# Stores, small constants and weight folding around the modulation stage of a hybrid encoder layer

## The chip, the cores and the metric

The kernel runs on one core of a Trainium2 chip. The metric is the device time of one execution in microseconds. Of the kernel before there are three timed runs, with a median of 2102.57 us (2102.38 to 2103.07). A profiled execution is shown beside them.

The engines are named as the profile names them: PE is TensorE (matmuls; PEld its weight loads), DVE is VectorE, ACT is ScalarE, POOL is GpSimd, and SP is the engine that issues most transfers. A DMA issue of an engine is written SPq or POOLq.

## What is computed

The reference is one layer of an encoder, run for two sequences of 1024 rows and 1024 columns. Cut to what matters:

```python
mod = silu(c) @ w_ada + b_ada                       # w_ada is 1024 x 6144
sh1, sc1, ga1, sh2, sc2, ga2 = split(mod, 6)
h = rmsnorm(x, g_mix) * (1 + sc1) + sh1
z = h @ w_in                                        # q_lat 256, kv_lat 128, k_pe 64, f_in 512
mix = concat(mla(q_lat, kv_lat, k_pe), fourier(f_in)) @ w_out
x = x + ga1 * mix
h2 = rmsnorm(x, g_ffn) * (1 + sc2) + sh2
y = x + ga2 * ((silu(h2 @ w_gate) * (h2 @ w_up)) @ w_down)      # then a final rmsnorm
```

The latent attention uses w_uq (256 to 4 heads of 128 + 64), w_ukv (128 to 4 heads of 128 + 128) and the gains g_q_lat and g_kv_lat. The kernel folds these weights into each other first.

## The kernel before

The kernel works in stages, and the change lies in the first. Everything is float32; a product of two large operands is done as three matmuls (mm3, L78 to L80) of a rounded high part and a remainder, which split (L62, L63) makes with a copy on ACT and a subtraction on DVE.

**The modulation stage.** w_ada's columns for shift and scale of the first norm (2048 of them) are read in eight chunks of 128 rows, 1 MB each (mod_load, L207), and mod_mm (L216) multiplies each with silu(c) into one PSUM bank. Chunks 0, 1, 3, 4 and 7 go through two wada tiles, the others through tiles that later work uses under other names (hh0, hh1). When the eighth chunk is multiplied, mod_row (L221) copies the sum, mod_vecs (L144 to L156) transposes it and adds bias and gain with twelve small DVE operations, and the first shift and scale vectors (sh1, s1) are there. flip (L381, L384) then transposes the normalised rows of x and applies them on ACT: hf, split into hh and hl. Nothing of the main work can start before that.

Between the chunks the stage prepares weights:
- fold_q (L238, L239) multiplies parts of w_uq and w_ukv into wq, fold_pe (L258) adds the rotary columns, and wq is stored to DRAM (wq_d, L260, issued by POOL);
- fold_out (L251, L253) multiplies the value part of w_ukv with w_out for one head, in two halves; heads 0 and 1 here, stored to wo_d by POOL (L254);
- prep_wcs (L336 to L346) folds the Fourier part of w_in (wfT, four loads of 512 KB) with a constant table;
- wz_split splits the other part of w_in (two loads of 896 KB, wz0 and wz1);
- norm (L365, L368) of the first rows: squares on ACT, a reciprocal root on POOL (rstd, L102 to L109), the scaling on DVE.

Small constants come one by one: cmask, cT (the conditioning), gkvr (one row of 128 read for all 128 partitions), gq, bT, gT. silu(c) is stored to DRAM too (sc_d, L197, POOL).

**The pairs.** Then eight pairs of row blocks follow: zproj (two products with wz, its rotary part with the tables ropec and ropes), latents (transposes), fourier_in (two products with wcs), flip of the next pair, evenodd (sums and differences on POOL, L397), norm of the pair after next. A generator, extras, puts other work between their steps, one step at each next(more): the fold_out of heads 2 and 3 (its weights loaded with L244; stored by SP), then the eight chunks of w_ada's gate columns (mod_load, mod_mm), then the products with the gates.

**What sets the order.** A tile framework schedules the instructions of each engine; each engine works in its own order. SP's transfers use eight completion semaphores in turn, so that each transfer's issue waits for the landing of the one eight before it, and for whatever still uses the tile that it fills. A tile with a tag is one buffer under several names: wq lies in hl0, which later holds the first hl; wuqT in hh0. The pool of PSUM has eight banks, taken in turn.

The later stages (attention, output product, the feed-forward products) are not touched.

Of the kernel before, what the change touches and what calls it, by code (L numbers as in the profile page):

```python
# [21 lines left out]
P = 128  # L22
D = 1024
# [29 lines left out]
def hybrid_encoder_kernel(ctx: ExitStack, tc: tile.TileContext, a: dict):  # L53
# [39 lines left out]
    nc.sync.dma_start(cmask, a["cmask"])  # L93
# [49 lines left out]
    def mod_vecs(mr, bank, bT, gT, bcol, gi, sv, shv):  # L143
        pt = bank().rearrange("p (a b) -> p a b", a=4)  # L144
        for c in range(4):
            nc.tensor.transpose(pt[:, c, :], mr[:, c * P : (c + 1) * P], ident)
        for s in range(2):
            for j in range(2):
                nc.vector.tensor_tensor(
                    out=shv[s][:, 4 * j : 4 * j + 4], in0=pt[:, :, 32 * j + s],  # L150
                    in1=bT[:, bcol + 4 * j : bcol + 4 * j + 4], op=ALU.add)
                nc.vector.tensor_tensor(
                    out=sv[s][:, 4 * j : 4 * j + 4], in0=pt[:, :, 64 + 32 * j + s],
                    in1=bT[:, bcol + 8 + 4 * j : bcol + 12 + 4 * j], op=ALU.add)
            nc.vector.tensor_scalar(out=sv[s], in0=sv[s], scalar1=1.0, scalar2=None, op0=ALU.add)
            nc.vector.tensor_tensor(out=sv[s], in0=sv[s], in1=gT[:, gi, :], op=ALU.mult)  # L156
# [7 lines left out]
    with ExitStack() as st:  # L164
# [25 lines left out]
        cT = w.tile([P, NC, 2], F32, name="cT")  # L190
        scT = w.tile([P, NC, 32], F32, name="scT")
        bT = w.tile([P, 48], F32, name="bT")
        gT = w.tile([P, 2, NC], F32, name="gT")
# [30 lines left out]
        def fold_loads():  # L224
            wukT = w.tile([P, HEADS, KVL], F32, tag="lh", name="wukT", bufs=2)
            nc.sync.dma_start(wukT, a["wukT"])
            nc.sync.dma_start(wuqT, a["wuqT"])
            gkvr = w.tile([P, KVL], F32, tag="t1", name="gkvr", bufs=2)
            nc.sync.dma_start(gkvr, a["gkvr"].partition_broadcast(P))
            gq = w.tile([P, 3], F32, name="gq")  # L230
            nc.sync.dma_start(gq, a["gq"])
            return wukT, gkvr, gq

        def fold_q(wukT, gkvr, gq):
# [12 lines left out]
        def fold_out(h, wo2, wuvT, gq):  # L247
            for g in range(2):
                gs = slice(512 * g, 512 * g + 512)
                ps = bank()  # L250
                nc.tensor.matmul(ps, wuvT[:, h, :], wo2[:, h % 2, gs], start=True, stop=True)  # L251
# [4 lines left out]
        def fold_pe(wpe, gq):  # L256
# [3 lines left out]
            nc.gpsimd.dma_start(wq_d, wq)  # L260
# [11 lines left out]
        def extras():  # L272
# [97 lines left out]
        def flip(k, g):  # L370
# [11 lines left out]
            for c in range(2):  # L382
                cc = 2 * g + c
                nc.scalar.activation(hf[:, cc], pt[:, c], AF.Identity, bias=sh1[s][:, cc : cc + 1], scale=s1[s][:, cc : cc + 1])  # L384
# [84 lines left out]
        fq = fold_loads()  # L469
        gq = fq[2]  # L470
        wt = [mod_load(c, cols0, wada_tile()) for c in range(2)]
        fold_q(*fq)
# [3 lines left out]
        wo2 = wo_load(0, wide("hf", (P, 2, D)))  # L476
# [7 lines left out]
        for q in range(4):  # L484
            wf.append(w.tile([P, 4, 256], F32, tag=("eoh0", "eol0", "eoh1", "eol1")[q], name="wf", bufs=1))
            nc.sync.dma_start(wf[q], a["wfT"][:, :, 256 * q : 256 * q + 256])
        fold_out(0, wo2, wuvT, gq)
        fold_out(1, wo2, wuvT, gq)
        fold_pe(wpe, gq)
        mod_mm(0, 2, wt[0])  # L490
        mod_mm(0, 3, wt[1])
# [6 lines left out]
        wz0 = wz_load(0, wide("hf", (P, 4 * 512)))  # L498
        mod_mm(0, 4, wt[0])
# [5 lines left out]
        wf.clear()  # L505
# [3 lines left out]
        mod_vecs(mod_row(0), bank, bT, gT, 0, 0, s1, sh1)  # L509
# [8 lines left out]
        nc.sync.dma_start(ropec, a["ropec"])  # L518
        nc.sync.dma_start(ropes, a["ropes"])
# [1148 lines left out]
def _layout(i):  # L1668
# [10 lines left out]
    for s in range(2):  # L1679
# [5 lines left out]
        "cT": c.reshape(2, NC, P).transpose(2, 1, 0),  # L1685
# [3 lines left out]
        "wfT": w_in[:, DZ:].T.reshape(4, P, D).transpose(1, 0, 2),  # L1689
# [4 lines left out]
        "gq": np.concatenate([sq["g_q_lat"].reshape(2, P).T, sq["g_kv_lat"].reshape(KVL, 1)], 1), "gkvr": sq["g_kv_lat"],  # L1694
        "w4": w4t, "w_out": sq["w_out"], "wgu": wgu, "w_down": sq["w_down"], "g_final": np.asarray(i["g_final"]),
    }
    return {k: np.ascontiguousarray(v) for k, v in r.items()}
# [19 lines left out]
```

## Time and profile before

| | |
|---|---|
| median of three runs | 2102.57 us |
| profiled execution, whole | 2103.97 us |
| its span, first to last instruction | 2102.2 us |
| mean granted PE clock | 0.99 |
| PE busy over the span | 2035.1 us, 97% |
| read and written in HBM | 259.47 and 122.49 MB |

The span is what the profile's windows divide; 1.8 us of the execution lie around it. A row of the timeline has the start and the duration in us, the engine and line, the operation, the tiles (out<-in), shapes and count, and in brackets how long the engine stood idle before and what ended that. A float32 matmul counts twice in it. A row of the windows has the window, its length, then for PE, PEld, DVE, ACT and POOL the busy us and count, then the granted clock of PE (1.00 is full speed), the busy share of the 16 DMA engines and GB/s.

### The profile page before, as it was taken

The page shows a single profiled execution, that of the slowest core. Times are in us where ns is not written, and L with a number is a line of the kernel's source. Part 1 is how long each engine was busy: PE and PEld are TensorE (multiplying, and loading weights), DVE is VectorE, ACT ScalarE, POOL GpSimd, SP SyncE. Part 2 cuts the span into 40 slices and gives each one's busy share as a digit, 9 for nine tenths or more (in the row PEclk, how much of TensorE's full clock was granted, in tenths as well). Part 3 has the DMA queues.
Part 4 walks back from the last instruction along what each step waited for, and adds up shares of the span by engine and source line. Part 5 has one row for each costly group of instructions (what it writes and reads, how often), then busy time and mean ns, then how long its engine had stood idle before and what let it go on. Part 6 is the DMA issues. An engine that isn't in the chain of part 4 may idle for free. (4 is left out here: it accounts for less than half of the span.)

```text
span 2102.2 us, 28839 instructions
## 1 busy us (share of the span) xinstructions
PE 2035.1 (97%) x10044; PEld 1667.4 (79%) x10044; DVE 1403.6 (67%) x2088; ACT 902.3 (43%) x1764; POOL 832.7 (40%) x1027
## 2 busy tenths in 40 slices
PE   6999999999999989999999999999999999999998
PEld 3788777888888877888888888877788888888876
DVE  3657766766777667767677666776756566567674
ACT  2766534455555555233323355453233233336441
POOL 1555111111313314878778610334554454420142
PEclk8999999999999999999999999999999999999999
DMA  9685795544643465455455487674332232258672
GB/s 370 206 260 172 258 314 174 131 101 101 157 109 125 146 212 203 165 185 193 168 180 197 159 269 261 212 238 160 116 125 101 76 126 100 76 167 284 226 227 93
DMA packets 187103, 375.49 MB, mean 179 GB/s; under 512 B 19341, under 2 KB 60941, under 8 KB 183885
## 3 DMA queue, kind: packets, MB, share of 16 engines
q1 hardware_dynamic: 168460, 316.09, 45.1%
q0 software_dynamic: 18496, 57.55, 9.1%
q8 instruction: 79, 1.29, 0.3%
q14 instruction: 68, 0.55, 0.1%
HBM read 259.47 MB, written 122.49 MB: 182 GB/s over the span
## 5 line engine op out<-in xcount | busy, mean ns | idle before, releaser
L78 PE MATMUL bank<-H,wh 128*128 128x512 f32 x1232 | 492.7, 400 | 9.2 <-ACT val L1397 4.5
L80 PE MATMUL bank<-H,wl 128*128 128x512 f32 x1232 | 486.7, 395 | 1.9 <-DVE wl L63 1.9
L79 PE MATMUL bank<-H,wh 128*128 128x512 f32 x1232 | 485.0, 394 | 0.2 <-DVE H L63 0.2
L138 DVE TENSOR_TENSOR val<-bank,val 128x512 f32<-128x512 f32 x244 | 167.0, 689 | 194.9 <-PE bank L80 188.0
L78 PEld LDWEIGHTS bank<-H,wh 128*128 128x128 f32 x1232 | 232.0, 188 | 66.1 <-DVE val L138 5.9
L80 PEld LDWEIGHTS bank<-H,wl 128*128 128x128 f32 x1232 | 232.1, 188 | 62.4 <-DVE wl L63 2.6
L79 PEld LDWEIGHTS bank<-H,wh 128*128 128x128 f32 x1232 | 231.8, 188 | 55.7 <-DVE H L63 0.6
L63 DVE TENSOR_TENSOR wl<-draw,wh 128x512 fp32r<-128x512 f32 x286 | 201.9, 741 | 87.5 <-ACT wh L62 87.0
L62 ACT CAST wh<-draw 128x512 fp32r<-128x512 f32 x286 | 168.4, 619 | 159.9 <-PE bank L79 83.8
L138 POOL TENSOR_TENSOR val<-val 128x512 f32<-128x512 f32 x58 | 84.1, 1456 | 368.3 <-DVE val L1498 189.2
L79 PE MATMUL bank<-wl,wh 128*128 128x512 f32 x572 | 223.8, 391 | 3.2 <-DVE wl L63 3.2
L62 ACT CAST wh<-rgu 128x512 fp32r<-128x512 f32 x172 | 106.7, 621 | 270.7 <-PE bank L79 214.2
L78 PE MATMUL bank<-wh 128*128 128x512 f32 x572 | 222.7, 389 | 0.0
L80 PE MATMUL bank<-wh,wl 128*128 128x512 f32 x572 | 222.7, 389 | 0.0
L62 ACT CAST wh<-val 128x512 fp32r<-128x512 f32 x133 | 82.3, 622 | 279.3 <-PE bank L79 250.9
L63 DVE TENSOR_TENSOR wl<-val,wh 128x512 fp32r<-128x512 f32 x133 | 137.8, 1038 | 89.1 <-ACT wh L62 89.0
L135 POOL TENSOR_TENSOR val<-rgu 128x512 f32<-128x512 f32 x84 | 124.2, 1478 | 124.9 <-DMA rgu<-in_wgu_dram 105.4
L63 DVE TENSOR_TENSOR wl<-rgu,wh 128x512 fp32r<-128x512 f32 x172 | 165.3, 962 | 4.8 <-ACT wh L62 4.6
L79 PEld LDWEIGHTS bank<-wl,wh 128*128 128x128 f32 x572 | 107.3, 188 | 28.7 <-DVE wl L63 6.8
L78 PEld LDWEIGHTS bank<-wh 128*128 128x128 f32 x572 | 107.4, 188 | 23.0 <-ACT wh L62 0.3
L80 PEld LDWEIGHTS bank<-wh,wl 128*128 128x128 f32 x572 | 107.4, 188 | 21.9
L135 POOL TENSOR_TENSOR val<-val 128x512 f32<-128x512 f32 x89 | 120.1, 1366 | 1.3
(354 smaller groups left out, 4053.4 us busy)
## 6 DMA issues: line engine op xcount, KB each, us to landing
rgu<-in_wgu_dram SPq DMA_DIRECT2D x86, 512.0 KB
draw<-s_d SPq DMA_DIRECT2D x143, 256.0 KB
s_d<-val POOLq DMA_DIRECT2D x88, 256.0 KB, 4.0
draw<-t_d SPq DMA_DIRECT2D x88, 256.0 KB
s_d<-val SPq DMA_DIRECT2D x66, 256.0 KB
draw<-in_w_down_dram SPq DMA_DIRECT2D x55, 256.0 KB
wada<-in_w_ada_dram SPq DMA_DIRECT2D x13, 1024.0 KB
xt<-in_x_dram SPq DMA_DIRECT2D x16, 512.0 KB
```

The costliest lines, as they stand in the source:

```text
L62: here["a"] = nc.scalar.copy(hi, src).ins
L63: here["v"] = nc.vector.tensor_tensor(out=lo, in0=src, in1=rd(hi), op=ALU.subtract).ins
L78: nc.tensor.matmul(out, lh, rh, start=first, stop=False, skip_group_check=cont)
L79: nc.tensor.matmul(out, lh, rl, start=False, stop=False, skip_group_check=cont)
L80: here["t"] = nc.tensor.matmul(out, ll, rh, start=False, stop=last, skip_group_check=cont).ins
L135: return eng.tensor_tensor(out=out, in0=x, in1=y, op=ALU.subtract).ins
L138: eng.tensor_tensor(out=out, in0=x, in1=y, op=ALU.add)
```

## The change

All of it lies in the first stage.

- **Constants.** cT, gq, bT, gT and gkvr are laid side by side on the host (gkvr repeated for the 128 partitions) and come in one transfer, pk, 128 x 211 floats, third on SP's queue. cmask is loaded later.
- **Stores.** The stores of sc_d, wq_d and wo_d move from POOL's queue to SP's, behind the load of the eighth chunk: two of wo_d and wq_d ahead of wz1 and of the second pair's x, the other six of wo_d, ropec, ropes, sc_d and cmask behind.
- **Folds.** fold_out for heads 2 and 3 runs between the chunks; the second half of w_out is loaded ahead of the fourth chunk. extras loses these steps, so that each of its later steps comes one next(more) earlier. The eight results lie in tiles of their own until they are stored.
- **wfT** is laid out so that each of its four loads reads 4 KB runs, where it read 1 KB runs; the last two loads come after the fourth chunk's.
- **Vectors.** mod_vecs has six DVE operations in place of twelve (in both places that call it). One of the eight hf of the first pair is done on DVE instead of ACT.

```diff
-    nc.sync.dma_start(cmask, a["cmask"])
...
         for s in range(2):
-            for j in range(2):
-                nc.vector.tensor_tensor(
-                    out=shv[s][:, 4 * j : 4 * j + 4], in0=pt[:, :, 32 * j + s],
-                    in1=bT[:, bcol + 4 * j : bcol + 4 * j + 4], op=ALU.add)
...
+            for k, v in enumerate((shv[s], sv[s])):
                 nc.vector.tensor_tensor(
...
-            nc.vector.tensor_scalar(out=sv[s], in0=sv[s], scalar1=1.0, scalar2=None, op0=ALU.add)
-            nc.vector.tensor_tensor(out=sv[s], in0=sv[s], in1=gT[:, gi, :], op=ALU.mult)
+            nc.vector.scalar_tensor_tensor(out=sv[s], in0=sv[s], scalar=1.0, in1=gT[:, gi, :], op0=ALU.add, op1=ALU.mult)
...
+        pk = w.tile([P, 211], F32, name="pk")
...
-        nc.sync.dma_start(cT, a["cT"])
         nc.vector.memset(scT, 0.0)
-        nc.scalar.activation(scT[:, :, 0:2], cT, AF.Silu)
-        nc.gpsimd.dma_start(sc_d, scT)
...
             nc.sync.dma_start(wuqT, a["wuqT"])
-            nc.sync.dma_start(gkvr, a["gkvr"].partition_broadcast(P))
-            nc.sync.dma_start(gq, a["gq"])
+            nc.sync.dma_start(pk, a["pk"])
+            nc.scalar.activation(scT[:, :, 0:2], cT, AF.Silu)
...
-                so = stile("so")
-                nc.vector.tensor_scalar(out=so, in0=ps, scalar1=gq[:, 2:3], scalar2=None, op0=ALU.mult)
-                (nc.gpsimd if h < 2 else nc.sync).dma_start(wo_d[:, h, gs], so)
+                nc.vector.tensor_scalar(out=outs[g], in0=ps, scalar1=gq[:, 2:3], scalar2=None, op0=ALU.mult)
+                folded.append((wo_d[:, h, gs], outs[g]))
...
-            nc.gpsimd.dma_start(wq_d, wq)
...
             cols1 = [(2 * D, D), (5 * D, D)]
-            wo2 = wo_load(1, wada_tile().rearrange("p a b -> p (a b)").rearrange("p (a b) -> p a b", a=2))
-            yield
-            fold_out(2, wo2, wuvT, gq)
             wt = mod_load(0, cols1, wada_tile())
             yield
-            fold_out(3, wo2, wuvT, gq)
             yield
...
+                if k == 0 and cc == 1:
+                    nc.vector.tensor_scalar(out=hf[:, cc], in0=pt[:, c], scalar1=s1[s][:, cc : cc + 1],
+                                            scalar2=sh1[s][:, cc : cc + 1], op0=ALU.mult, op1=ALU.add)
+                    continue
...
-        wt = [mod_load(2, cols0, wide("hh1")), mod_load(3, cols0, wada_tile())]
+        wt = [mod_load(2, cols0, wide("hh1"))]
         nc.sync.dma_start(c2, a["c2"])
...
+        wf_load(0)
+        wf_load(1)
+        wo2.append(wo_load(1, wide("hl1", (P, 2, D))))
+        wt.append(mod_load(3, cols0, wada_tile()))
...
         for i in range(4):
             prep_wcs(i, wf[i // 2])
+        wf_load(2)
+        wf_load(3)
+        mod_mm(0, 3, wt[1])
         wt = [mod_load(4, cols0, wada_tile()), mod_load(5, cols0, wide("hh1"))]
-        nc.sync.dma_start(bT, a["bT"])
-        nc.sync.dma_start(gT, a["gT"])
+        fold_out(2, wo2[1], wuvT, (w.tile([P, 512], F32, tag="gah0", name="so"), stile("so")))
+        fold_out(3, wo2[1], wuvT, (stile("so"), stile("so")))
         norm(0)
         wz0 = wz_load(0, wide("hf", (P, 4 * 512)))
+        for i in range(4, 8):
+            prep_wcs(i, wf[i // 2])
...
         wt = [mod_load(6, cols0, wide("hh0")), mod_load(7, cols0, wada_tile())]
+        for dst, so in folded[:2]:
+            nc.sync.dma_start(dst, so)
+        nc.sync.dma_start(wq_d, wq)
         wz1 = wz_load(4, wide("hl1", (P, 4 * 512)))
-        for i in range(4, 8):
-            prep_wcs(i, wf[i // 2])
...
+        x_load(1)
+        for dst, so in folded[2:]:
+            nc.sync.dma_start(dst, so)
+        nc.sync.dma_start(ropec, a["ropec"])
+        nc.sync.dma_start(ropes, a["ropes"])
+        nc.sync.dma_start(sc_d, scT)
+        nc.sync.dma_start(cmask, a["cmask"])
         wz_split(0, wz0)
         mod_mm(0, 6, wt[0])
         mod_mm(0, 7, wt[1])
-        mod_vecs(mod_row(0), bank, bT, gT, 0, 0, s1, sh1)
+        mr = w.tile([P, 4, 256], F32, tag="eol1", name="modrow", bufs=1).rearrange("p a b -> p (a b)")[:, :512]
+        nc.vector.tensor_copy(mr, mods.pop(0))
+        mod_vecs(mr, bank, bT, gT, 0, 0, s1, sh1)
...
-        nc.sync.dma_start(ropec, a["ropec"])
-        nc.sync.dma_start(ropes, a["ropes"])
```

On each engine the instructions after this stage and its pairs come in the same order as before, but for a few neighbours that change places.

More of the change, by code (lines that the diff above doesn't have):

```diff
@@ L189, in hybrid_encoder_kernel @@
         zoc = [w.tile([P, NC, ZOW], F32R, name=f"zoc{i}") for i in range(2)]
-        cT = w.tile([P, NC, 2], F32, name="cT")
+        pk = w.tile([P, 211], F32, name="pk")
+        cT = pk[:, 0:16].rearrange("p (a b) -> p a b", b=2)
+        gq = pk[:, 16:19]
+        bT = pk[:, 19:67]
+        gT = pk[:, 67:83].rearrange("p (a b) -> p a b", a=2)
+        gkvr = pk[:, 83:211]
         scT = w.tile([P, NC, 32], F32, name="scT")
-        bT = w.tile([P, 48], F32, name="bT")
-        gT = w.tile([P, 2, NC], F32, name="gT")
-        nc.sync.dma_start(cT, a["cT"])
         nc.vector.memset(scT, 0.0)
-        nc.scalar.activation(scT[:, :, 0:2], cT, AF.Silu)
-        nc.gpsimd.dma_start(sc_d, scT)
         mods = {}
@@ L227, in fold_loads, with fold_q @@
             nc.sync.dma_start(wuqT, a["wuqT"])
-            gkvr = w.tile([P, KVL], F32, tag="t1", name="gkvr", bufs=2)
-            nc.sync.dma_start(gkvr, a["gkvr"].partition_broadcast(P))
-            gq = w.tile([P, 3], F32, name="gq")
-            nc.sync.dma_start(gq, a["gq"])
-            return wukT, gkvr, gq
-        def fold_q(wukT, gkvr, gq):
+            nc.sync.dma_start(pk, a["pk"])
+            nc.scalar.activation(scT[:, :, 0:2], cT, AF.Silu)
+            return wukT
+        def fold_q(wukT):
             for h in range(HEADS):
@@ L245, in wo_load, with fold_out @@
             return t
-        def fold_out(h, wo2, wuvT, gq):
+        folded = []
+        def fold_out(h, wo2, wuvT, outs):
             for g in range(2):
@@ L468, in hybrid_encoder_kernel @@
         cols0 = [(0, 2048)]
-        fq = fold_loads()
-        gq = fq[2]
+        wukT = fold_loads()
         wt = [mod_load(c, cols0, wada_tile()) for c in range(2)]
-        fold_q(*fq)
+        fold_q(wukT)
         nc.gpsimd.memset(lw, 0.0)
@@ L475, in hybrid_encoder_kernel @@
         nc.sync.dma_start(wuvT, a["wuvT"])
-        wo2 = wo_load(0, wide("hf", (P, 2, D)))
+        wo2 = [wo_load(0, wide("hf", (P, 2, D)))]
         wpe = w.tile([P, 2, HEADS * ROPE], F32, tag="lh", name="wpe", bufs=2)
```

27 lines of the change are left out of this document (14 added, 13 removed).

## Prediction

> **What bounds the kernel now.** I read the page first, then the busy time by stage, then what TensorE (PE) waited for.
>
> ```profile
> span 2102.2 us, 28839 instructions
> PE 2035.1 (97%) x10044; PEld 1667.4 (79%) x10044; DVE 1403.6 (67%) x2088; ACT 902.3 (43%) x1764; POOL 832.7 (40%) x1027
> ```
>
> PE is the bound over the whole, but 97% is an average. By stage (window, its length, busy us of PE, PEld, DVE, ACT, POOL, granted clock, DMA share, GB/s):
>
> ```profile
> 0.00:56.00 56.00, 34.67 (x173) 20.29 (x174) 19.14 (x59) 14.09 (x37) 6.39 (x20) 0.85 0.94 366
> 69.20:80.90 11.70, 7.22 (x35) 4.05 (x34) 9.13 (x21) 9.00 (x22) 9.58 (x25) 1.00 0.30 90
> 80.90:225.00 144.10, 143.26 (x912) 122.17 (x912) 94.51 (x188) 86.04 (x214) 74.86 (x157) 1.00 0.71 223
> 700.00:2102.00 1402.00, 1371.53 (x6029) 1111.55 (x6027) 943.73 (x1182) 537.36 (x953) 642.56 (x652) 0.99 0.51 174
> ```
>
> Two holes lie where the change works: 21.3 us without PE in the first 56, with the DMA share at 0.94, and 4.5 us between 69.2 and 80.9, with the DMA idle and three engines busy. From 80.9 PE is full (143.26 of 144.10), and late 98% full. So what PE is spared early ends up whole in the time. PE's longest wait in the first stage, from the waits (us, times, longest), and the matmuls of the last chunk, from the timeline (start, us):
>
> ```profile
> PE bank L216 <- DMA wide<-in_w_ada_dram: 7.6, 2, 6.2
> ```
>
> ```profile
> 48.63 1.93 PE L216 MATMUL bank<-wada,scT 128*32 128x512 f32 x8 [0.57 <-DMA wada<-in_w_ada_dram]
> ```
>
> The modulation's eighth chunk of w_ada landed at 48.63, and everything after hangs on it. The first stage is a queue of bytes ahead of that chunk, and I count what the change does to it. The DMA's rate in pieces of the stage, and the sizes (KB each) of what moves:
>
> ```profile
> 5.00:8.00 3.00, 1.62 (x6) 1.36 (x6) 0.00 (x0) 0.00 (x0) 0.53 (x1) 1.00 0.57 160
> 7.50:47.90 40.40, 26.93 (x138) 14.91 (x138) 16.31 (x43) 10.43 (x30) 4.45 (x11) 0.87 1.03 407
> 12.00:21.00 9.00, 7.86 (x22) 2.42 (x19) 2.25 (x5) 0.00 (x0) 1.08 (x2) 1.00 1.02 417
> 21.00:24.00 3.00, 3.00 (x19) 0.61 (x18) 0.91 (x2) 0.00 (x0) 1.10 (x2) 1.00 1.07 345
> 28.00:31.00 3.00, 1.71 (x14) 1.74 (x15) 0.50 (x3) 0.69 (x3) 0.00 (x0) 0.95 1.07 366
> 31.00:34.00 3.00, 3.00 (x16) 3.00 (x16) 1.76 (x7) 1.58 (x7) 0.00 (x0) 0.50 1.05 434
> 40.00:47.90 7.90, 1.77 (x8) 0.20 (x8) 3.00 (x4) 4.08 (x6) 1.73 (x6) 0.56 1.01 420
> ```
>
> ```profile
> wo_d<-so POOLq DMA_DIRECT2D x4, 256.0 KB, 7.7
> wada<-in_w_out_dram SPq DMA_DIRECT2D x1, 1024.0 KB
> wq_d<-wq POOLq DMA_DIRECT2D x1, 768.0 KB, 8.3
> sc_d<-scT POOLq DMA_DIRECT2D x1, 128.0 KB, 6.9
> ```
>
> **Part 1, bytes ahead of the last chunk: -2.3 us.** Four wo_d stores (1024 KB), wq_d (768) and sc_d (128) leave: 1920 KB. The second half of w_out (1024 KB), which came after the chunk, now comes before it. The small constants are a wash (six transfers of 109 KB against pk, 128 x 211 floats, 105.5 KB). Net -900 KB = 0.92 MB, at the 407 GB/s of 7.5 to 47.9: 2.3 us. The Trainium skill ("DMA: Bandwidth & Descriptors", section "Where 436 GB/s comes from") says that about 358 GB/s binds transfers between HBM and SBUF; by that the bytes would be worth 2.6 us. The trace disagrees, with 420 GB/s over 7.9 us.
>
> ```profile
> 0.73 0.39 SPq L93 DMA_DIRECT2D cmask<-in_cmask_dram  x1
> 1.63 0.43 SPq L226 DMA_DIRECT2D wukT<-in_wukT_dram  x1
> 2.58 0.43 SPq L229 DMA_DIRECT2D gkvr<-in_gkvr_dram  x1
> 3.53 0.91 SPq L207 DMA_DIRECT2D wada<-in_w_ada_dram  x2
> ```
>
> **Part 2, the start of the queue: -0.9 us.** SP spends 0.73 to 1.63 on cmask and cT before its first large load. In the changed order wukT is SP's first transfer.
>
> **Part 3, the hole behind gkvr: -1.4 us, between 0 and -1.85.** From 5 to 8 us the queue moved 160 GB/s with the engines 57% busy, although 1 MB loads had been issued since 3.53: 3 x (1 - 160/417) = 1.85 us lost. gkvr (one row read for 128 partitions) and gq stand there. They go; pk, contiguous per partition, takes their place. Whether they cause the hole no row proves, so 0 stays an end; I take three quarters.
>
> **Part 4, slow stretches: -0.5 us, between 0 and -0.9.** 21 to 24 (345) and 28 to 31 (366) lie below 417: 3 x (72 + 51)/417 = 0.9 us. In the first the stores mix with loads; in the second wfT is read in 1 KB runs, which become 4 KB.
>
> The chunk lands 5.1 us sooner (3.2 to 5.9). Waits in the queue: each SP transfer waits for the eighth before it to land, and a wada tile for PE's matmuls on what it held. At 2.5 us a MB the chunk before it in that tile is multiplied at some 30 us (rival 5), and the eighth chunk's turn comes at 38.8: I expect nothing to run dry. The folds of heads 2 and 3 now stand among these matmuls, on a PE that idles 21 us here; cost 0.
>
> **Part 5, behind the chunk.**
>
> ```profile
> 53.84 1.48 ACT L384 ACTIVATE hf<-bank,sh,s 128x256 f32<-128x256 f32 x3 [8.45 <-DVE s L152]
> 55.20 0.62 ACT L62 CAST hh<-hf 128x512 fp32r<-128x512 f32 x1
> 55.85 0.69 DVE L63 TENSOR_TENSOR hl<-hf,hh 128x512 fp32r<-128x512 f32 x1 [1.64 <-ACT hh L62]
> 55.87 0.47 PE L78 MATMUL bank<-wz_h,hh 128*128 128x448 f32 x1 [0.50 <-ACT hh L62]
> 57.12 1.80 ACT L62 CAST wz_h<-wide 128x896 fp32r<-128x896 f32 x2
> 61.72 1.09 ACT L365 ACTIVATE junk<-xt 128x1024 bf16<-128x1024 f32 x1
> ```
>
> Twelve small DVE operations become six, and one of the eight hf moves from ACT (1.48/3 = 0.49 us) to DVE, which waited 1.64 there. The first s is then the fourth of these operations instead of the eighth: I take **-0.5 us** (0 to -0.8).
>
> The stores moved behind the chunk now precede wz1 and x(1). 512 + 768 KB at the mixed 345 GB/s are 3.8 us, wz1 (896 KB) 2.2, x(1) 2.5. Counted from the chunk, wq_d lands at +3.8, wz1 at +6.0, x(1) at +8.5. They are needed at +6.7 (hl shares wq's tile: 55.85 - 48.63 - 0.5), +8.0 (57.12) and +12.6 (61.72): covered, by 2.0 us at the tightest. The other six stores, ropec and ropes come behind; the first use of ropec, after zproj, is 2 us later still. Cost 0, and each us beyond the cover costs one.
>
> **Part 6, the folds that leave 69 to 81.**
>
> ```profile
> 55.29 0.89 SPq L355 DMA_DIRECT2D xt<-in_x_dram  x2
> 74.63 0.22 POOL L102 TENSOR_SCALAR rs_v<-ms 128x2 f32<-128x2 f32 x1
> 74.93 1.88 PE L251 MATMUL bank<-wada,wuvT 128*128 128x512 f32 x4
> 76.55 0.19 POOL L109 TENSOR_TENSOR rs_r<-rs_w,rs_y 128x2 f32<-128x2 f32 x1
> 77.96 1.88 PE L251 MATMUL bank<-wada,wuvT 128*128 128x512 f32 x4
> 80.83 0.39 PE L78 MATMUL bank<-wcs_h,eoh 128*128 128x256 f32 x1 [0.98 <-DVE ll L63]
> 80.84 1.18 ACT L62 CAST eoh<-eo 128x512 fp32r<-128x512 f32 x2
> 87.60 2.77 POOL L397 TENSOR_TENSOR eo<-hf 128x512 f32<-128x512 f32 x2 [6.27 <-DVE eol L63]
> 88.56 1.03 PE L381 MATMUL bank<-ident,xt 128*128 128x128 f32 x8
> 89.53 1.07 PE L216 MATMUL bank<-wada,scT 128*32 128x512 f32 x8
> ```
>
> 3.76 us of PE (two L251 rows) go, and the gate matmuls (1.07 us a chunk) come one step earlier. fourier_in, now at 80.83, would start at 80.83 - 3.76 - 0.98 (the wait on ll: it takes another bank) + 1.07 = 77.2 in the old clock; it and zproj(1, 0) take 88.56 - 80.83 = 7.7, to 84.9. But the changed order moves more: x(2)'s loads, issued at 55.29, now stand on SP behind the first pair's ckv and lat stores, and its squares, its rstd (here 74.63 to 76.74, 2.1 us) and its scaling follow the eo work. My estimate in the old clock: eoh ends at 82.5 (82.0, and the copy to zs that now goes ahead), DVE's second eol at 83.3, two eo at 86.0 (2.77), rstd at 88.1, the first scaled rows at 88.9. The third pair's transposes (88.56 now) can't start before about 89.1, so a PE wait of nearly 4 us takes the folds' place. By then one more gate chunk is done: **-1.0 us**, between +0.5 (the chain some 1.5 us longer) and -3.8 (all of it). Behind, the order on PE is the same up to where the gate chunks are made up.
>
> Sum: 2.3 + 0.9 + 1.4 + 0.5 + 0.5 + 1.0 = 6.6. Against the profiled execution (2103.97 us, 1.8 around its span) that is 2097.4; the median of the runs is 1.4 lower, 2102.57, and 6.6 below it is **2096.0 us**.
>
> **The rivals.**
> 1. The folds' whole 3.8 us comes off, if x(2)'s chain ends earlier than I trace it: 2102.57 - 5.1 - 0.5 - 3.8 = 2093.2. For it, DVE loses four evictions just there; against it, the order.
> 2. The hole and the slow stretches stay, since they belong to the queue's start and to the shapes and not to these transfers: 3.2 + 0.5 + 1.0 = 4.7, 2097.9.
> 3. PE's new idle stretch before the third pair's transposes, about 3.7 us (from 85.4, half a gate chunk after 84.9, to 89.1), halves its clock.
>
> ```profile
> 29.29 7.22 PE L336 MATMUL bank<-c,wf 128*128 128x128 f32 x48 [3.24 <-DMA wf<-in_wfT_dram]
> ```
>
> Such an idle 3.24 us was followed by clock 0.50 in 31 to 34: some 3.2 us at half speed, 1.6 lost, 2097.6. Against: 69.2 to 80.9 has 4.5 us idle in pieces at clock 1.00. The Trainium skill ("TensorE: Matmul & The Clock Gate", section "Part 1: The HAM clock gate") says that one idle window of about 3.4 us, on a free-running grid, halves the clock. The rows at 29.29 and 31 agree.
> 4. Slower: the stores choke the queue. The first hl waits for wq_d, which decides once its 1.31 MB (two wo_d and wq_d) take over 6.7 us, below 196 GB/s; the whole gain is lost at 13.3 us, 99 GB/s; at 80 GB/s it would be 16.4, +3.1, 2105.7. No row shows stores alone; the nearest, 345 with stores mixed in, speaks against it.
> 5. The change doesn't shorten the queue, because the eighth chunk is issued late: its tile is free when the fourth chunk is multiplied, which now stands on PE behind four preps and the folds of heads 2 and 3. It decides if that comes after some 37 us (38.8 less an estimated 1.5 between issue and first bytes); from there each us costs one. At 3 us late the time is 2099.0.
>
> **How the numbers follow.** Forecast 0.55; rivals 0.15, 0.14, 0.09, 0.04, 0.03. About 0.2% (4.2 us, below 2098.4) is what a measurement of this kernel can tell from no change. The forecast lies beyond that in 51 of its 55 hundredths, rival 1 wholly, 2 and 3 by half: faster 0.78, same 0.17, slower 0.05. The range, 2092.5 to 2099.8, takes in rivals 1, 2 and 3 and leaves out the far ends.
>
> **What would show it.** In the changed profile the eighth chunk's L211 matmul at 43 to 44 us (48.63 now); over 400 GB/s from 4 us on without a dip at 5 to 8; first z matmul at 50 to 51; hl not waiting for wq_d; the third pair's transposes waiting on DVE's xt for 2 to 4 us. Wrong if the DMA share falls below 0.9 before the chunk, if wz1 or a store ends a wait, or if PE from there to the end takes longer than 2102.2 - 48.6 = 2053.6 us.

## The result and the profile after

| | before | after |
|---|---|---|
| median of seven runs | 2102.38 us (2098.69 to 2103.11) | 2108.78 us (2106.47 to 2111.82) |
| ratio after to before | | 1.0034 (95% interval 1.0024 to 1.0044) |
| profiled execution, span | 2103.97, 2102.2 us | 2108.78, 2107.0 us |

The change makes the kernel 0.34% slower. The forecast was 2096.0 us, so what was expected and what came lie 12.8 us apart.

First the busy time by stage of the kernel after (window, its length, busy us of PE, PEld, DVE, ACT and POOL, granted clock, DMA share, GB/s):

```profile
69.20:80.90 11.70, 11.04 (x62) 8.48 (x61) 7.09 (x15) 9.48 (x22) 4.42 (x9) 0.74 0.88 244
80.90:225.00 144.10, 136.61 (x842) 112.84 (x841) 89.19 (x172) 82.75 (x204) 79.31 (x158) 0.99 0.63 199
```

In 80.9 to 225 PE was busy 143.26 us before and is busy 136.61 now: 6.65 us of new standing, in the stage that the prediction called full. In 69.2 to 80.9 PE stands less (11.04 us busy, 7.22 before), but the clock fell to 0.74.

Markers in the timeline show where the lead goes. The eighth chunk's product, the first z product, the second pair's first transpose, and the first z product of the last pair of the stage, in the kernel after:

```profile
44.06 1.94 PE L211 MATMUL bank<-wada,scT 128*32 128x512 f32 x8 [0.55 <-DMA wada<-in_w_ada_dram]
...
51.31 0.49 PE L78 MATMUL bank<-wz_h,hh 128*128 128x448 f32 x1
...
66.19 0.30 PE L370 MATMUL bank<-ident,xt 128*128 128x128 f32 x1 [0.80 <-DVE xt L357]
...
220.71 0.37 PE L78 MATMUL bank<-wz_h,hh 128*128 128x448 f32 x1
```

and the last two of them in the kernel before (the first two are in the prediction, 48.63 and 55.87):

```profile
70.78 0.30 PE L381 MATMUL bank<-ident,xt 128*128 128x128 f32 x1 [1.34 <-DVE xt L368]
...
214.39 0.37 PE L78 MATMUL bank<-wz_h,hh 128*128 128x448 f32 x1
```

After is ahead by 4.57, 4.56 and 4.59 us, and then behind by 6.32. So the first stage gives 4.6 of the 5.6 us that parts 1 to 5 promised, and between 66 and 221 us 10.9 us are lost, although 3.76 us of folds have left this stretch. The loss comes at two places: at the first z product of each of the eight pairs after is ahead by 4.56 and 5.63 us, then behind by 1.83, 1.83 and 0.65, and then by 5.90, 5.94 and 6.32. Behind it the two profiled executions differ by 1.5 us more, in after's favour, with halved clock in other places; that part isn't followed.

What PE waited for between 66 and 225 us, after and before (us in total, times, longest):

```profile
PE bank L370 <- DVE xt L357: 7.6, 5, 3.2
PE bank L431 <- DVE lat L416: 1.2, 2, 1.0
PE bank L211 <- DMA wada<-in_w_ada_dram: 0.8, 1, 0.8
PE bank L431 <- POOL lat L415: 0.7, 1, 0.7
```

```profile
PE bank L438 <- POOL lat L422: 1.9, 2, 1.2
PE bank L381 <- DVE xt L368: 1.6, 2, 1.3
PE bank L78 <- DVE ll L63: 1.0, 1, 1.0
```

The waits for xt, the scaled rows of x, grew from 1.6 to 7.6 us. The timeline of PE after has them, and two more things, around 70, 85 and 157 us; its last row stands below it as it was before:

```profile
70.58 1.91 PE L370 MATMUL bank<-ident,xt 128*128 128x128 f32 x8
73.28 1.94 PE L211 MATMUL bank<-wada,scT 128*32 128x512 f32 x8
...
83.03 1.05 PE L211 MATMUL bank<-wada,scT 128*32 128x512 f32 x2
87.15 0.41 PE L370 MATMUL bank<-ident,xt 128*128 128x128 f32 x2 [3.07 <-DVE xt L357]
87.49 1.04 PE L211 MATMUL bank<-wada,scT 128*32 128x512 f32 x2
89.72 1.05 PE L211 MATMUL bank<-wada,scT 128*32 128x512 f32 x4
...
101.38 1.05 PE L211 MATMUL bank<-wada,scT 128*32 128x512 f32 x4
104.59 1.05 PE L211 MATMUL bank<-wada,scT 128*32 128x512 f32 x4 [0.79 <-DMA wada<-in_w_ada_dram]
...
157.06 0.32 PE L370 MATMUL bank<-ident,xt 128*128 128x128 f32 x1 [3.18 <-DVE xt L357]
157.62 1.76 PE L370 MATMUL bank<-ident,xt 128*128 128x128 f32 x7 [0.25 <-DVE xt L357]
159.31 2.56 PE L299 MATMUL bank<-wada,lw 128*64 128x512 f32 x8
```

```profile
160.20 1.94 PE L310 MATMUL bank<-wada,lw 128*64 128x512 f32 x8
```

Read in order. **Waits:** 3.07 us at 84 (the one that was forecast), 0.79 at 104, 3.18 + 0.25 at 154. The two lists add up to 10.3 and 4.5 us; without the first wait of each (0.80 and 1.34), which lies ahead of the first transpose, 9.5 and 3.2: 6.3 more. **Split chunks:** a gate chunk is four products on 32 columns each (8 records) that take 1.07 us together in before. Here one stands in three pieces (83.03, 87.49, 89.72) and one in two (101.38, 104.59), and each piece takes 1.05 us by itself: 3.15 us more. **Halved clock:** eight xt transposes take 1.91 instead of 1.04, a whole gate chunk 1.94 instead of 1.07, the products with the gates 2.56 instead of 1.94; with the transposes of lat between, some 2.7 us around 70 and 1.7 around 157. 6.3 + 3.15 + 4.4 = 13.9 of the 14.7 (10.9 + 3.76) that are to be explained.

The wait at 154 has its reason on POOL. After, in the order of the chain (the last of the squares on ACT, POOL's work, the scaling on DVE), then before (the root of a norm runs from rs_v<-ms to rs_r):

```profile
149.97 0.20 ACT L354 ACTIVATION_READ_ACCUMULATOR junk<-xt 128x1 f32 x1
...
150.53 2.54 POOL L390 TENSOR_TENSOR eo<-hf 128x512 f32<-128x512 f32 x2 [3.03 <-DVE eol L63]
153.16 0.54 POOL L101 TENSOR_SCALAR rs_v<-ms 128x2 f32<-128x2 f32 x1
...
155.93 0.20 POOL L108 TENSOR_TENSOR rs_r<-rs_w,rs_y 128x2 f32<-128x2 f32 x1
156.16 1.41 DVE L357 TENSOR_SCALAR xt<-xt,rs_r 128x1024 f32<-128x1024 f32 x2 [1.70 <-POOL rs_r L108]
```

```profile
148.60 0.20 POOL L109 TENSOR_TENSOR rs_r<-rs_w,rs_y 128x2 f32<-128x2 f32 x1
151.46 2.98 POOL L397 TENSOR_TENSOR eo<-hf 128x512 f32<-128x512 f32 x2 [2.67 <-DVE eol L63]
```

Before, the root is done at 148.8, and only then the two differences eo wait 2.67 us for DVE. After, eo comes first in POOL's order, waits 3.03 us, and the root, whose squares ACT had ended at 150.2, is done at 156.1. POOL takes its work in the order laid out; what waits in front of the root holds it. Over all pairs of after, two roots stand behind both differences where before they stood ahead of them: the third pair's, and this one.

### The profile page after: what moved, and what is told of

It is laid out like the page before. It is cut to its first block, busy times and chain, and to the rows that moved or that the text cites. A ratio compares the mean times of both kernels' runs of the same rounds, so it can differ in the third digit from the quotient of the medians.

```text
span 2107.0 us, 28822 instructions
## 1 busy us (share of the span) xinstructions
PE 2042.7 (97%) x10044; PEld 1668.2 (79%) x10044; DVE 1406.9 (67%) x2077; ACT 903.1 (43%) x1763; POOL 831.7 (39%) x1021
## 5 line engine op out<-in xcount | busy, mean ns | idle before, releaser
L78 PEld LDWEIGHTS bank<-H,wh 128*128 128x128 f32 x1232 | 232.1, 188 | 69.6 <-ACT val L1408 6.7
L137 POOL TENSOR_TENSOR val<-val 128x512 f32<-128x512 f32 x58 | 83.2, 1442 | 368.3 <-DVE val L1509 188.7
L63 DVE TENSOR_TENSOR wl<-val,wh 128x512 fp32r<-128x512 f32 x133 | 134.5, 1013 | 86.2 <-ACT wh L62 86.2
L1009 DVE TENSOR_REDUCE mx<-ps_s 128x1 f32<-128x1024 f32 x64 | 78.2, 1221 | 63.3 <-PE ps_s L1004 63.2
```

The costliest lines, as they stand in the source:

```text
L63: here["v"] = nc.vector.tensor_tensor(out=lo, in0=src, in1=rd(hi), op=ALU.subtract).ins
L78: nc.tensor.matmul(out, lh, rh, start=first, stop=False, skip_group_check=cont)
L137: eng.tensor_tensor(out=out, in0=x, in1=y, op=ALU.add)
L1009: nc.vector.tensor_reduce(out=mx, in_=ps, axis=AX.X, op=ALU.max)
```

## The experiments

**The theory:** the engines' orders decide. extras lost a step, so every gate step comes one next(more) earlier. The framework laid out each engine's order anew, with the root of two norms behind eo and gate chunks in pieces, and the loads of the third pair's x late. **Rivals:** a supply (x's chain, the gate chunks' loads) bounds the pairs, so that an earlier PE only waits for it; or the halved clock alone costs the time.

**1. Gate steps where they were.** After, with one empty step:

```diff
             cols1 = [(2 * D, D), (5 * D, D)]
+            yield
             wt = mod_load(0, cols1, wada_tile())
```

> The kernel after, with one more empty step ahead of the gate chunks, so that each gate step comes at the step where it came before the change. Theory (the order decides): from 66 us on the time of after is lost where the engines' fixed orders put one thing behind another. The steps moved one earlier put the gate's sums and products ahead of the norm of the pair after next; POOL then has both differences of eo ahead of that norm's reciprocal root, and PE stands 3.2 us at 153.9 us and runs the next 2.6 us of its work at half clock: 5.1 us in all; and the second split gate chunk (1.05 us and 0.8 us of wait for its load) goes, the first is split in two instead of three (1.05 us). 2108.8 - 5.1 - 1.9 - 1.1 = 2100.7; no PE wait for xt near 154 us, the one near 84 us (3.1 us) stays. Rival (a supply bounds the pairs): x, the squares, the root and the gate chunks can't come faster than in before, so that a PE that starts 4.6 us earlier only waits for them; with other steps the wait turns up at another place: 2106 to 2109. Rival (the clock): the halved clock alone costs the time, and comes where its windows fall: 2105 to 2109, with as many halved stretches as in after.

Measured: 2099.3 us, ratio to before 0.9986 (0.9977 to 0.9994). One empty step turns the loss of 0.34% into a gain of 0.14%. On POOL the one later root is ahead of its differences again, the third pair's is not, and in the waits from 66 to 225 us xt stands once, at 84:

```profile
PE bank L371 <- DVE xt L358: 4.0, 1, 4.0
PE bank L432 <- DVE lat L417: 1.0, 1, 1.0
PE bank L432 <- POOL lat L416: 1.0, 1, 1.0
```

**2. The step alone, in the kernel before.**

```diff
             fold_out(2, wo2, wuvT, gq)
+            fold_out(3, wo2, wuvT, gq)
             wt = mod_load(0, cols1, wada_tile())
-            yield
-            fold_out(3, wo2, wuvT, gq)
             yield
```

> The kernel before, with the folds of heads 2 and 3 in one step of extras instead of two, so that the gate steps come one earlier, as in after; nothing else is changed. Theory (the order decides): the wait at 154 us of after comes from this alone and appears here too, 3.2 us of standing and 1.9 us of halved clock, at about 150 to 160 us: 2102.4 + 5.1 = 2107.5. Rival (a supply bounds the pairs): without the lead of 4.6 us PE does not catch up with the supply, 2101.5 to 2103.5. Rival (the clock): no reason for a change, 2101 to 2104.

Measured: 2111.82 us, ratio 1.0044 (1.0032 to 1.0056): as slow as after within the intervals, with nothing else of the change in it. The same wait, to the hundredth, and behind it the products with the gates at half clock (3.30 us; 2.56 in after, 1.94 in before):

```profile
158.74 0.30 PE L380 MATMUL bank<-ident,xt 128*128 128x128 f32 x1 [3.18 <-DVE xt L367]
159.31 1.26 PE L380 MATMUL bank<-ident,xt 128*128 128x128 f32 x7 [0.27 <-DVE xt L367]
160.50 3.30 PE L309 MATMUL bank<-wada,lw 128*64 128x512 f32 x8
```

It cost 4 us more than was expected. Its first gate chunks also come a step earlier than their loads (1.63 us of wait at 90, 1.35 us for ll at 79), which the expectation left out; by the first z product of the last pair (222.25 us, 214.39 in before) 7.9 us are lost, where 5.1 were expected. So the lead isn't what makes the wait at 154: this PE had almost none (first z product at 55.42 us, 55.87 in before).

**3. The norm first.** After, with norm called ahead of evenodd in each pair:

```diff
+            norm(2)
             evenodd(1)
-            norm(2)
...
+            if k + 2 < nk:
+                norm(k + 2)
             if k + 1 < nk:
                 evenodd(k + 1)
-            if k + 2 < nk:
-                norm(k + 2)
```

> The kernel after, with norm of the pair after next called ahead of evenodd of the next pair, in each pair; the gate steps stay early. Theory (the order decides): the root of the norm then stands ahead of the differences of eo on POOL from the third norm on, and the wait at 154 us goes with its halved clock (5.1 us); the norm of the third pair keeps its place, so the wait at 84 us (3.1 us) and the split gate chunks (3.2 us) stay: 2108.8 - 5.1 = 2103.7. eo comes later by the time of the root, up to 2 us, which PE sees only if fourier_in waits: up to 2106. Rival (a supply bounds the pairs): the wait moves, 2107 to 2109. Rival (the clock): 2105 to 2109.

Measured: 2102.36 us, ratio 1.0002 (0.9994 to 1.0011). 6.4 us below after, 5.1 expected. The gate steps are as early as in after; what moved is the norm, its squares, root and scaling. Of the two late roots the one at 154 is ahead of its differences again, the third pair's is not:

```profile
148.56 0.22 POOL L101 TENSOR_SCALAR rs_v<-ms 128x2 f32<-128x2 f32 x1 [1.71 <-ACT junk L354]
...
152.80 2.51 POOL L390 TENSOR_TENSOR eo<-hf 128x512 f32<-128x512 f32 x2 [2.13 <-DVE eol L63]
```

**4. A gate chunk in one transfer.** After, with this in mod_load:

```diff
+            if len(cols) == 2:
+                nc.sync.dma_start(
+                    wt.rearrange("p a b -> p (a b)").rearrange("p (k n) -> p k n", k=2),
+                    a["w_ada"][c * P : (c + 1) * P, :].rearrange("p (k m) -> p k m", k=2)[:, :, 2 * D :])
+                return wt
```

> The kernel after, with each gate chunk of w_ada loaded in one transfer of 1 MB instead of two of 512 KB. Theory (the order decides): a chunk's four products, which run side by side in 1.06 us when they stand together, take 1.05 us for each piece when the order splits them; here none is split, so 2.1 us for the chunk split in three and 1.05 us for the one split in two go, and perhaps the 0.8 us of wait for the second load: 2108.8 - 3.2 = 2105.6, down to 2104.8; both waits for xt stay (3.1 and 3.2 us). Rival (a supply bounds the pairs): the pieces filled time in which PE would wait anyway, so the waits for xt grow by as much: 2108 to 2110. Rival (the clock): the same, 2107 to 2110.

Measured: 2105.76 us, ratio 1.0022 (1.0013 to 1.003), 3.0 us below after, 3.2 expected, but the two intervals overlap. No chunk is split, and both long waits for xt stay (4.0 and 3.18 us). The first of them grew from 3.07, and behind it the clock is at half from 84.7 to 91.5 us, which it isn't in after; by the first z product of the last pair only 1.5 us are left (219.24 instead of 220.71). So the pieces took time, but a part of it comes back as waiting and as slow clock, and the 3.15 us aren't shown as their price.

**5. The norm first and the third pair's x early.** Experiment 3, and x_load(2) taken out of the first pair and put behind cmask's load:

```diff
         nc.sync.dma_start(cmask, a["cmask"])
+        x_load(2)
```

> The kernel of the experiment with the norm called ahead of evenodd, and the loads of the third pair's x issued right behind cmask instead of behind the first pair's latents, so that the third pair's norm stands ahead of the second pair's differences on POOL as well. Theory (the order decides): against the experiment without the early loads (2102.4) the wait of the third pair's transposes goes (2.6 to 3.1 us) with the halved clock behind it (85.6 to 89.0 us, 1.7 us), and one split of a gate chunk of the three (1.05 us): 2102.4 - 2.6 - 1.7 - 1.0 = 2097.1. Rival (a supply bounds the pairs, here x(2)'s chain from load to scaled rows): the chain ends where it did, and PE waits for other things until then: 2101.5 to 2103.

Measured: 2097.47 us, ratio 0.9976 (0.9966 to 0.9985), 4.9 us below experiment 3, 5.3 expected. The wait at 84 us is gone; the halved stretch at 69 us is longer (68.6 to 78.9). So that wait, too, was made by the order: in after, the two loads of x(2) stand on SP behind the first pair's stores,

```profile
70.14 0.38 SPq L344 DMA_DIRECT2D xt<-in_x_dram  x1
...
73.03 0.56 SPq L436 DMA_DIRECT2D lat_d<-ll  x1
73.68 0.60 SPq L344 DMA_DIRECT2D xt<-in_x_dram  x1
```

where before issued both at 55.29.

**6. Both, with one transfer a chunk.** The edits of 3, 4 and 5 together.

> As the experiment with the norm first and the third pair's x early, and each gate chunk in one transfer, which leaves no chunk split. The gate steps stay early, as in after. Theory (the order decides): all three losses of after are gone. 2097.1 as worked out for the kernel with two transfers, less 1.05 us for its one split chunk and 0.7 us of wait for a second load: 2095.3. That is near the forecast for the change itself. Rival (a supply bounds the pairs): 2101 to 2103. Between them, 2097 to 2100, if the transfer of 1 MB comes later than its first half did and PE waits for it.

Measured: 2097.5 us, ratio 0.9984 (0.9975 to 0.9993): no gain over experiment 5, where 2 us were expected; the expectation had 2097 to 2100 for the case that PE waits for the larger transfer, and this case came. No chunk is split, but one comes late and the clock is halved when it comes:

```profile
76.36 1.94 PE L216 MATMUL bank<-wada,scT 128*32 128x512 f32 x8 [3.43 <-DMA wada<-in_w_ada_dram]
78.23 0.58 PE L78 MATMUL bank<-wcs_h,eoh 128*128 128x256 f32 x1
```

Its tile's 1 MB is now waited for whole, where half of it let PE begin. Here a supply does bound.

**7. Folds of heads 2 and 3 back in extras.** After, with all else of the change kept:

```diff
             cols1 = [(2 * D, D), (5 * D, D)]
+            wo2.append(wo_load(1, wada_tile().rearrange("p a b -> p (a b)").rearrange("p (a b) -> p a b", a=2)))
+            yield
+            fold_out(2, wo2[1], wuvT, (stile("so"), stile("so")))
+            for dst, so in folded[4:6]:
+                nc.sync.dma_start(dst, so)
             wt = mod_load(0, cols1, wada_tile())
             yield
+            fold_out(3, wo2[1], wuvT, (stile("so"), stile("so")))
+            for dst, so in folded[6:]:
+                nc.sync.dma_start(dst, so)
             yield
...
-        wo2.append(wo_load(1, wide("hl1", (P, 2, D))))
...
-        fold_out(2, wo2[1], wuvT, (w.tile([P, 512], F32, tag="gah0", name="so"), stile("so")))
-        fold_out(3, wo2[1], wuvT, (stile("so"), stile("so")))
```

> The kernel after, with the folds of heads 2 and 3 and the load of their weights left in extras, as in before (their stores go out there too); all else of the change is kept, and the gate steps come at before's steps. Theory (the order decides): the prologue's gain alone, 4.6 us and 0.4 us for 1 MB that leaves the queue ahead of the eighth chunk's 2.5 us; the folds' 3.8 us stay on PE, but where PE would wait for the third pair's xt (4.0 us in the kernel with later gate steps), so they cost less than 1 us there. Against the kernel with later steps (2099.3): 2097.5 to 2100. Rival (the folds' time comes off whole when they move to the prologue, as the kernel with later steps has it): 2099.3 + 3.8 - 2 = 2101 to 2103.

Measured: 2098.16 us, ratio 0.9987 (0.9977 to 0.9997), as the theory had it and not the rival. The eighth chunk's product comes at 42.07 us, zproj(1, 0) at 73.9, and then the wait for xt takes 4.24 us, with the clock at half behind it (81.2 to 88.1 us): with the folds on PE or without them, x(2) is late.

**8. The constants alone, in the kernel before.** pk is packed as in after:

```diff
-    nc.sync.dma_start(cmask, a["cmask"])
...
-        nc.sync.dma_start(cT, a["cT"])
...
             nc.sync.dma_start(wuqT, a["wuqT"])
-            nc.sync.dma_start(gkvr, a["gkvr"].partition_broadcast(P))
-            nc.sync.dma_start(gq, a["gq"])
+            nc.sync.dma_start(pk, a["pk"])
+            nc.scalar.activation(scT[:, :, 0:2], cT, AF.Silu)
+            nc.gpsimd.dma_start(sc_d, scT)
...
-        nc.sync.dma_start(bT, a["bT"])
-        nc.sync.dma_start(gT, a["gT"])
...
         nc.sync.dma_start(ropes, a["ropes"])
+        nc.sync.dma_start(cmask, a["cmask"])
```

> The kernel before with the constants in one transfer, third on SP's queue, and cmask late; stores, folds, wfT and vectors as before. By the prediction's parts 2 and 3: SP's first large load comes 0.9 us sooner and the hole of 160 GB/s at 5 to 8 us goes (1.4 us, at most 1.85), so that the eighth chunk is multiplied at 48.6 - 2.3 = 46.3 us (45.9 at best), and the order behind is that of before: 2101.5 - 2.3 = 2099.2. Rival (the hole belongs to the queue's start and not to gkvr): 47.7 us and 2100.6. Rival (the queue is bound by its bytes alone, as the stores still stand in it): 48.6 us and 2101.5.

Measured: 2099.49 us, ratio 0.9991 (0.9982 to 1.0). Its eighth chunk and its window from 5 to 8 us:

```profile
47.03 1.93 PE L215 MATMUL bank<-wada,scT 128*32 128x512 f32 x8 [0.57 <-DMA wada<-in_w_ada_dram]
```

```profile
5.00:8.00 3.00, 2.64 (x11) 2.34 (x12) 1.16 (x4) 1.50 (x2) 0.00 (x0) 1.00 0.82 323
```

1.60 us of 2.3 came; the dip rose from 160 to 323 GB/s and not to 417. In this kernel the order behind is before's, and the lead is kept: 1.9 us at the first z product of the last pair (212.48, 214.39 in before), 1.8 by the medians (2101.29 to 2099.49), though the interval of the ratio just reaches 1.

**9. Experiment 7 with the norm first and x(2) early.** The edits of 3, 5 and 7 together.

> The kernel with the folds of heads 2 and 3 left in extras, and in it the norm called ahead of evenodd and the third pair's x loaded behind cmask. All the rest of the change is kept. Theory (the order decides): the eighth chunk's product at 42.1 us and zproj(1, 0) at 73.9 us as in the kernel with the folds in extras, 8.0 us ahead of the kernel with the constants alone (81.9 us, 2099.5 us), and no wait for xt behind it, since the order of the pairs is that of before: 2099.5 - 8.0 = 2091.5. Rival (a supply bounds the pairs): the third pair's xt is ready no sooner than some 82 us, so PE waits about 3 us at 79 us as it does in the kernel with the folds in extras (4.2 us): 2094.5 to 2096. Rival (the clock halves at 69 to 79 us whatever stands there): 2095 to 2096.

Measured: 2096.18 us (2090.17 to 2098.15), ratio 0.9967 (0.9956 to 0.9979): the fastest median. On PE its pairs have before's order, with no chunk split, and no wait for xt is left at 79 us:

```profile
41.55 1.93 PE L211 MATMUL bank<-wada,scT 128*32 128x512 f32 x8 [0.54 <-DMA wada<-in_w_ada_dram]
...
77.10 0.37 PE L78 MATMUL bank<-wz_h,hh 128*128 128x448 f32 x1
...
81.92 1.03 PE L378 MATMUL bank<-ident,xt 128*128 128x128 f32 x8
```

The profiled execution, 2090.17 us, is the lowest of eight; the median lies 4.7 us over the expected 2091.5. zproj(1, 0) comes at 77.1 us and not at 73.9, as PE stands 0.9 us for a fold's eviction and runs at half clock from 66.2 to 69.6: 4.8 us ahead of experiment 8 instead of 8.0, which makes 2094.7. Experiments 9 and 10 ran on another chip, where before took 2102.49 us instead of 2101.29; by the ratios, 9 lies 5.0 us below 8, as the 4.8 say. So the supply rival's wait didn't come, and of the clock rival's price a part did.

**10. Idle products.** Experiment 5, with two products of 128x512 of the unit matrix and ropec in each of the first two steps of extras; their results go nowhere:

```diff
+            def idle_products():
+                for _ in range(2):
+                    ps = bank()
+                    nc.tensor.matmul(ps, ident, ropec.rearrange("p a b -> p (a b)"), start=True, stop=True)
+
             yield
+            idle_products()
             yield
+            idle_products()
```

> The kernel with the norm first and the third pair's x early (2097.5 us), and in it four products of 128x512 of the unit matrix with ropec, in the two steps of extras and at the places on PE at which before folds heads 2 and 3; nobody reads their results. They cost what a fold costs, 0.94 us each, 3.8 us in all, of which some 1.5 us fall into waits that are there anyway (0.67 and 1.12 us). Theory (the standing PE of 65 to 71 us halves the clock from 68.6 to 78.9 us): with them PE keeps its clock, and what ran at half there gets it back: the latents' transposes 0.4 + 0.1 + 0.5 us, the xt transposes 0.9, the gate chunk 0.9, fifteen of the products of fourier_in 1.2, in all 3.9 us: 2097.5 + 3.8 - 1.5 - 3.9 = 2095.9, and no halved stretch between 65 and 85 us. Rival (the halved clock has another cause, as the prologue's work or the earlier start): 2097.5 + 2.3 = 2099.8, and the halved stretch is still there.

Measured: 2098.73 us, ratio 0.998 (0.997 to 0.9989), between the two. The halved stretch still begins (69.0 us, 68.6 in experiment 5), but ends at 75.8 and not at 78.9. So the products came too late to prevent it, and early enough to shorten it: 3.8 us of useless work cost 0.8 us by the ratios, whose intervals overlap, and 1.8 us in the traces at the first z product of the last pair (213.88, 212.07 in experiment 5). It settles no price for the clock.

Taken together: the order theory gave the sign of experiments 1 to 5, and within 1.5 us the time of 1, 3, 4, 5 and 7; in 2 its price was too low, in 6 and 9 too favourable. One point tells more than the time of one execution: the first z product of the last pair starts at 214.39 us in before, at 220.71 in after, and in experiments 1 to 10 at 213.88, 222.25, 215.70, 219.24, 212.07, 212.28, 212.48, 212.48, 208.22 and 213.88. Behind it, where PE does the same work but for a few neighbours that change places, the twelve traces take 1880.2 to 1887.8 us, which is more scatter than most of these experiments are worth. By this point experiment 3 gains 5.0 us (5.1 expected), but 4 only 1.5 of 3.2, and 5 only 3.6 of 5.3 over experiment 3. As the cause of a long wait the supply rival holds in experiment 6 alone; shorter waits for a chunk's load (0.7 to 1.6 us) stand in after and in experiments 2, 3 and 5. The clock rival fails as a cause of its own, as the halved stretch at 157 us goes wherever the wait ahead of it goes (experiments 1, 3, 5) and comes where it comes (2); as a part of a wait's price it stands.

## Why the prediction was wrong, step by step

**Bytes and slow stretches (parts 1 and 4): right.** From experiment 8 (47.03) to after (44.06) the chunk comes 2.97 us sooner, for a forecast of 2.3 + 0.5. The stores without the second half of w_out (experiment 7, 42.07) make 4.96 us; 1.97 MB at the 407 GB/s used are 4.8, and with part 4, which this kernel has too, 5.3. The two parts aren't told apart.

**Start and hole (parts 2 and 3): right in kind, too large.** 1.60 us instead of 2.3. SP issues wukT at 0.73 us instead of 1.63, as forecast; if these 0.9 us count whole, the hole gave 0.7 of 1.4. In after, 5 to 8 us still has 328 GB/s where over 400 were named as a sign.

**Vectors (part 5): nothing came of it.** From the chunk to the first z product it was 7.24 us before and is 7.25. z no longer waits for hh (0.50 before), but the xt transposes ahead of it run wholly at half clock:

```profile
44.06:51.31 7.25, 6.34 (x28) 4.33 (x28) 1.94 (x9) 2.14 (x5) 0.48 (x1) 0.50 1.01 367
```

In experiments 1, 3 and 7, with the same vectors, the clock is back at full at 45.6, 44.6 and 43.7 us, and the same stretch takes 6.00, 5.78 and 6.07 us. So what decides it is when the clock comes back, which the forecast left out; what the vectors alone are worth stays open.

**The folds that leave (part 6): the first wait was foreseen, and its price right** (3.07 us; 2 to 4 forecast), as the chain of x(2) came as traced: its root is done at 86.2 us, 88.1 forecast, with PE there 1.3 us sooner too. What failed is the sentence behind it: "Behind, the order on PE is the same up to where the gate chunks are made up", and with it the reading of 143.26 of 144.10 as a PE that stays full whatever comes. On PE the gate steps moved by one, and on POOL and DVE so did work that shares their queues with the norms. PE was full in before because each root ended some us ahead of its use (148.8 for transposes at 153.1), and that was a property of the order. For a gain of 1.0 us the runs show a loss: 3.18 us of wait at 154 with some 1.7 of halved clock behind it, 2.7 of halved clock around 70, and split chunks (3.15 by their rows). Experiments 2 and 1 put and take the larger part of it with that one step; experiment 3 takes the wait at 154 with the steps left early, and 5 the one at 84. The framework fixes each engine's order ahead of the run. The prediction followed it on PE and, for the third pair, on POOL and DVE, but not on POOL for the later pairs, where one root changed places; nor did it price a chunk in pieces, which PE's order has. (It also called the DMA idle between 69.2 and 80.9 us; its row has a share of 0.30.) The Trainium skill ("TensorEngine Tiling (Array Packing)", section "Key Properties") says that tiles of the array work independently, in parallel; the rows agree, with 1.07 us for four products side by side and 1.05 for a piece of them.

**Rival 3** (an idle stretch halves the clock) named the mechanism, but in after it works at 68 us, ahead of the wait that it was hung on, and again at 157; behind the wait at 84 itself the clock is halved in experiments 1, 3, 4 and 7 and not in after. **Rivals 4 and 5** did not occur: no store ends a wait of PE, and the eighth chunk was issued at 27.88 us (the 38.8 that rival 5 rests on is worked out nowhere). The sign named for being wrong did: from the chunk to the end PE took 2062.9 us, not 2053.6. No rival held what happened, since all of them took the order of the later pairs as given.

**Left open:** whether moving the folds of heads 2 and 3 gains anything at all. Experiment 9 (folds in extras) and 5 (folds in the prologue) lie at 0.9967 and 0.9976 with intervals that overlap. On the trace their 3.8 us fall partly into waits that stand there anyway, and experiment 9 is 3.9 us ahead of 5 at the first z product of the last pair, so nothing here speaks for moving them.

## What to carry to other kernels

A step that is taken out of a generator shifts every later step against the rest of the program; where a scheduler lays out the engines, compare the order of every engine, not of the bound one alone, and look for what now stands ahead of the instruction that feeds it. A full engine tells that its feeders were in time, not that they will be. A lead won early is only kept if the chains that feed the next stage (here load, squares, root, scaling) come ahead by as much.

## What the runs showed of the hardware

The clock of PE follows its busy share in windows of 3.41 us, with two bounds. In the twelve traces (before, after, ten experiments), without the last stretch of each, it fell from full to half 80 times, always behind a window with PE busy 53% or less, and it came back 80 times, always behind a window with 82% or more; 52 windows at half clock with 82% or less were followed by another. Between 44 and 53% it fell or didn't. In experiment 5:

```profile
65.20:68.61 3.41, 1.58 (x11) 0.96 (x9) 3.21 (x8) 0.39 (x1) 3.07 (x7) 1.00 0.00 0
68.61:72.02 3.41, 2.47 (x11) 2.10 (x12) 2.76 (x12) 2.99 (x8) 2.03 (x10) 0.50 0.38 62
72.02:75.44 3.42, 2.30 (x11) 1.25 (x9) 2.20 (x4) 3.42 (x8) 1.39 (x2) 0.50 0.91 284
75.44:78.85 3.41, 3.41 (x15) 2.42 (x12) 2.21 (x4) 3.41 (x7) 1.22 (x1) 0.50 1.06 320
78.85:82.26 3.41, 3.41 (x23) 2.40 (x22) 1.15 (x2) 0.46 (x3) 1.71 (x6) 1.00 1.04 332
```

1.58 of 3.41 us busy (46%), in standing of no more than 1.0 us at a time, halves the next window; 2.47 and 2.30 us busy (72 and 67%) don't bring the clock back; a full window does. The Trainium skill ("TensorE: Matmul & The Clock Gate", section "Part 1: The HAM clock gate") speaks of an idle window of about 3.4 us; here one that is half idle is enough. In experiment 8 the same standing falls so that its window has 53%, and the clock stays:

```profile
67.28:70.69 3.41, 1.79 (x14) 1.25 (x12) 2.70 (x6) 0.91 (x4) 3.00 (x10) 1.00 0.00 0
```

The windows don't start with the kernel (the clock comes back at 54.62 us in before, 51.38 in after, 49.12 in experiment 9, which are not whole windows apart), and which stretches are halved changes from trace to trace (in before at 337.9 to 341.3 us, in after nowhere near). It may be a part of what makes runs of one kernel differ by several us. That isn't shown, as there is one trace of each kernel; behind the first z product of the last pair the two with the least time at half clock (10.2 us before the last stretch; experiments 7 and 9) are the shortest, 1881.0 and 1880.2 us, but the six with 17.1 us take anything from 1882.5 to 1887.8.
